# Compressed value products of two pairs in one group at the head of the sums, and the norms' epsilon on VectorE, in a two-layer hybrid decoder

## The chip, the cores and the metric

The kernel runs on one core of a Trainium2 chip. A core has a matrix engine (TensorE, PE in the rows), VectorE (DVE), ScalarE (ACT), GpSimd (POOL) and SyncE (SP), which here only issues transfers. Matrix products are written to PSUM, which has eight banks of 128 partitions by 512 float32; everything else works in SBUF. The metric is device time of one execution in microseconds; lower is better.

## The reference, cut to what matters

Two layers over 512 tokens of width 1024. In each, a projection feeds three mixers (a gated spatial MLP, a retention and a sparse attention), their outputs are joined and projected back, and a layer norm follows; then a gated feed-forward part with a short convolution, and a second layer norm. Two places bear on the change, the sum of three attention branches and the layer norm:

```python
o_cmp = jnp.einsum('bgrqk,bkgd->bqgrd', p_cmp.astype(dt), v_cmp)
...
o = gb[..., 0:1] * o_cmp + gb[..., 1:2] * o_sel + gb[..., 2:3] * o_win

def layer_norm(x, g, b):
    mu = jnp.mean(xf, axis=-1, keepdims=True)
    var = jnp.mean(jnp.square(xf - mu), axis=-1, keepdims=True)
    y = (xf - mu) * lax.rsqrt(var + LN_EPS)
    return (y * g.astype(jnp.float32) + b.astype(jnp.float32)).astype(x.dtype)
```

The compressed branch has 31 keys (padded to 32); the other two have up to 512. There are eight heads of width 64 in two groups of four.

## The kernel before, in words

Most products are made as three products of rounded halves (`mm3`, lines 449 to 453; `tm`, 538 to 546), which keeps float32 accuracy. TensorE's program runs through input projection, attention with retention between, output projection, the feed-forward part and the next layer. A scheduler of the framework orders each engine's instructions from the traced order, by readiness and free tiles; what is wrapped in `pin` keeps its traced place on its engine. All PSUM tiles come from one pool `ps` of eight banks.

**Attention** (`attention`, line 1045). The heads go in four pairs `hp` of two heads `e`; pairs 0 and 1 share key group `g` = 0, pairs 2 and 3 group 1. A pair has eight units (b, i): branch b (0 selected, 1 window) and token tile i of four. For a unit, `scores` makes the products with the keys, the mask, maximum, exp, sum and scale; it runs two units ahead (LOOK = 2) and takes two banks for tiles 2 and 3. `transposes` turns the probabilities and copies them to SBUF. After tile 3 of a branch, `pv_mm` (1027 to 1042) multiplies with the values into one bank `po` for the pair: head 0 on columns 0 to 63 of the array, head 1 on 64 to 127, all 128 rows (line 1032). After branch 1 it adds the compressed branch (line 1039): 64 rows of `PC[g]`, the transposed probabilities of the pair's two heads of four (rows 0 to 63 for the even pair, 64 to 127 for the odd one), with `vcs`, the compressed values with zero rows for the other head. That closes the sum, and ScalarE copies it out (`YC`, 1042). `po` is taken at unit 0 of each pair. Between the steps of attention a generator `filler` gives TensorE other work: the retention's projections and chunks, in layer 0 also the conditioning products (`ada_bank`, line 327), later the first output products.

**Norms.** `stats` (line 1179) combines the tile's statistics on VectorE (`bn_aggr`, 1181), adds EPS on GpSimd (1182) and raises to the power -1/2 on GpSimd (1183). It is called 16 times: four token tiles, two norms, two layers. After the output projection, `normalize` (1185) subtracts and scales in one VectorE instruction, and `to_h` (430) transposes the tile for the next products. In layer 0 GpSimd also issues the transfers of the next layer's conditioning weights (line 341) in that time.

**The end** (lines 1371 to 1386). In layer 1 the last six row blocks of the down projection run tile by tile: for each tile t, TensorE makes two halves of 512 columns (the last tile: 512, 256, 256), `piece` (1351) gates, adds and takes statistics on VectorE, then `stats` and `norm_out` (1361): one subtract with gain over all 1024 columns (1363), multiply and add in halves (1366), each followed by a transfer to the output (1367). All of VectorE's instructions there are pinned in traced order.

Of the kernel before, what the change touches and what calls it, by code (L numbers as in the profile page):

```python
# [14 lines left out]
OP = mybir.AluOpType  # L15
# [4 lines left out]
D = 1024  # L20
NT = S // P
# [127 lines left out]
def tile_trunk(ctx, tc, I, tab, out, layers=L):  # L149
# [368 lines left out]
    for l in range(layers):  # L518
# [501 lines left out]
        def transposes(i, pp, PT):  # L1020
            for e in range(2):
# [2 lines left out]
                    T.transpose(pb[:, j * P:(j + 1) * P], pp[e][:, j * P:(j + 1) * P], ident)  # L1024
                A.copy(PT[e][:, i:i + 3 * i + 1:3, :], pb[:, :(i + 1) * P].rearrange("p (j q) -> p j q", q=P))  # L1025

        def pv_mm(hp, b, PT, po):

            g = hp // 2
            for j in range(NT):  # L1030
                for e in range(2):
                    T.matmul(po[64 * e:64 * e + 64, j * P:], VS[:, b, j, 64 * g:64 * g + 64],  # L1032
                             PT[e][:, 4 * j:4 * j + NT - j, :].rearrange("p a q -> p (a q)"),
                             start=(b == 0 and j == 0), stop=False, tile_position=(0, 64 * e))
            if b == 0:
                return
            rs = slice(64 * (hp % 2), 64 * (hp % 2) + 64)
            for e in range(2):
                T.matmul(po[64 * e:64 * e + 64, :], vcs[rs, g, e, :], PC[g][rs], start=False, stop=True,  # L1039
                         tile_position=(64 * (hp % 2), 64 * e))  # L1040
            YC[hp] = pool.tile([P, 512], F32, tag="yc", name="yc", bufs=2)
            A.copy(YC[hp], po)

        def attention():
            units = [(hp, b, i) for hp in range(4) for b in range(2) for i in range(NT)]
            LOOK = 2
            pend = {}
            PT = po = None
            for u, (hp, b, i) in enumerate(units):
                for v in range(u, min(u + LOOK + 1, len(units))):  # L1050
                    if v not in pend:
                        h_, b_, i_ = units[v]
                        if i_ == 0 and not b_:
                            pend[v], pend[v + NT] = scores0(h_)
                        else:
                            pend[v] = scores(*units[v])
                if i == 0:
                    PT = [big("pT").rearrange("p (a q) -> p a q", q=P) for _ in range(2)]
                    if b == 0:
                        po = ps()  # L1060
                yield
                transposes(i, pend[u], PT)
                pend[u] = None
                yield
                if i == NT - 1:
                    pv_mm(hp, b, PT, po)
                    if b:
                        yield ("pair", hp)
# [110 lines left out]
        def stats(t, st, nst, dve=loose):  # L1179
            mv = pool.tile([P, 4], F32, tag="mv", name="mv", bufs=4)  # L1180
            dve(V.bn_aggr(mv[:, 0:2], st[:, :nst, :]))  # L1181
            G.tensor_scalar(mv[:, 2:3], mv[:, 1:2], EPS, None, op0=OP.add)  # L1182
            G.tensor_tensor(mv[:, 3:4], mv[:, 2:3], mhalf[:, 0:1], op=OP.pow)
            return mv

# [174 lines left out]

        def norm_out(t, mv):

            pin(V.scalar_tensor_tensor(X[t], X[t], mv[:, 0:1], lgr, op0=OP.subtract, op1=OP.mult))
            for c0, c1 in ((0, 512), (512, D)) if t < NT - 1 else ((0, 512), (512, 768), (768, D)):
                c = slice(c0, c1)
                pin(V.scalar_tensor_tensor(X[t][:, c], X[t][:, c], mv[:, 3:4], lbr[:, c], op0=OP.mult, op1=OP.add))
                nc.sync.dma_start(out[0, t * P:(t + 1) * P, c], X[t][:, c])
# [56 lines left out]
```

## Time and profile before

| what | value |
|---|---|
| median of 3 runs | 1386.84 us (1384.04 to 1389.21) |
| profiled execution, its own time | 1387.29 us |
| span from first to last instruction | 1385.5 us |
| TensorE busy | 1344.4 us, 97% |
| VectorE busy | 871.7 us, 63% |
| ScalarE busy | 545.0 us, 39% |
| GpSimd busy | 193.6 us, 14% |
| mean granted clock of TensorE | 0.994 |

All times of the trace count from the first instruction. A matrix product's record runs from issue to a modelled end and overlaps its followers, so spacing is read from starts. A float32 product is two instructions (two passes). GpSimd's spans are rough.

### The profile page before, as it was taken

How to read it: one execution, taken by the hardware profiler on the slowest of the kernel's cores; microseconds unless marked ns; L12 is line 12 of the kernel's file. 1: busy time of each engine (PE TensorE's matmuls, PEld its weight loads, DVE VectorE, ACT ScalarE, POOL GpSimd, SP SyncE). 2: the span in 40 equal slices, each digit the busy share in tenths (PEclk: the TensorE clock that was granted, in tenths of full speed). 3: DMA queues.
4: the chain of work that ended last, by engine and by line, in shares of the span. 5: the costliest groups of instructions: out<-in, count | busy, mean ns of one | idle time of the engine just before them, and what ended most of it. 6: DMA issues, size and time to landing. Idle time of an engine off the chain costs nothing.

```text
span 1385.5 us, 19644 instructions
## 1 busy us (share of the span) xinstructions
PE 1344.4 (97%) x7741; PEld 1107.8 (80%) x7741; DVE 871.7 (63%) x1436; ACT 545.0 (39%) x998; POOL 193.6 (14%) x196
## 2 busy tenths in 40 slices
PE   5999999999999999999999999999999999999996
PEld 4798665679987878778889988877998888888885
DVE  6668443756697776943567677475665555674347
ACT  3435333553433343332424354565343334343220
POOL 0311220334121120000000024112400000000002
PEclk9999999999999999999999999999999999999998
DMA  9822555512596674423525231111223333332221
GB/s 301 230 80 69 167 165 149 174 47 77 163 291 213 213 247 145 132 89 100 158 46 132 64 107 50 43 47 39 84 77 94 105 91 122 105 123 91 91 91 61
DMA packets 182328, 168.91 MB, mean 122 GB/s; under 512 B 23588, under 2 KB 161948, under 8 KB 182236
## 3 DMA queue, kind: packets, MB, share of 16 engines
q1 hardware_dynamic: 174684, 141.18, 34.8%
q0 software_dynamic: 7552, 26.48, 5.7%
q8 instruction: 61, 1.00, 0.3%
q14 instruction: 31, 0.25, 0.1%
HBM read 163.44 MB, written 2.10 MB: 119 GB/s over the span
## 4 chain that ended last, share of the span: by engine, by line
PE 85%; DVE 6%; DMA 3%; ACT 2%; POOL 1%; SPq 1%; issue 1%; POOLq 0%; DVEq 0%; ACTq 0%
PE ps L451 19%; PE ps L453 19%; PE ps L452 19%; PE ps L544 4%; PE ps L545 4%; PE ps L546 4%; PE ps L1032 3%; PE ps L327 2%; PE ps L1024 2%; DMA a<-in_w_ada_dram 1%; PE ps L973 1%; PE ps L974 1%; DMA wraw<-in_w_up_dram 1%; DMA wraw<-in_w_in_dram 1%; PE ps L1039 1%
## 5 line engine op out<-in xcount | busy, mean ns | idle before, releaser
L125 ACT CAST whi<-wraw 128x1024 fp32r<-128x1024 f32 (+4 forms) x183 | 181.5, 996 | 391.1 <-PE ps L452 235.5
L127 DVE TENSOR_TENSOR wlo<-wraw,whi 128x1024 fp32r<-128x1024 f32 (+3 forms) x157 | 181.6, 1162 | 160.9 <-ACT whi L125 157.6
L453 PE MATMUL ps<-h2h,wlo 128*128 128x512 f32 (+1 forms) x736 | 278.3, 378 | 0.0
L452 PE MATMUL ps<-h2l,whi 128*128 128x512 f32 (+1 forms) x736 | 277.2, 377 | 0.0
L451 PE MATMUL ps<-h2h,whi 128*128 128x512 f32 (+1 forms) x736 | 277.1, 377 | 0.0
L452 PEld LDWEIGHTS ps<-h2l,whi 128*128 128x128 f32 x736 | 138.2, 188 | 28.7 <-issue 1.7
L451 PEld LDWEIGHTS ps<-h2h,whi 128*128 128x128 f32 x736 | 138.2, 188 | 28.4 <-ACT whi L125 2.5
L453 PEld LDWEIGHTS ps<-h2h,wlo 128*128 128x128 f32 x736 | 138.3, 188 | 26.1 <-issue 0.8
L544 PE MATMUL ps<-whi,hh 128*128 128x256 f32 (+1 forms) x448 | 132.0, 295 | 0.0
L545 PE MATMUL ps<-wlo,hh 128*128 128x256 f32 (+1 forms) x448 | 129.1, 288 | 0.0
L546 PE MATMUL ps<-whi,hl 128*128 128x256 f32 (+1 forms) x448 | 127.2, 284 | 0.0
L452 PE MATMUL ps<-wlo,pt 128*128 128x512 f32 x256 | 101.4, 396 | 0.0
L451 PE MATMUL ps<-whi,pt 128*128 128x512 f32 x256 | 101.2, 396 | 0.0
L544 PEld LDWEIGHTS ps<-whi,hh 128*128 128x128 f32 x448 | 85.4, 191 | 13.9 <-issue 11.3
L453 PE MATMUL ps<-whi,pt 128*128 128x512 f32 x256 | 90.4, 396 | 0.0
L545 PEld LDWEIGHTS ps<-wlo,hh 128*128 128x128 f32 x448 | 85.4, 191 | 5.6 <-issue 5.3
L127 POOL TENSOR_TENSOR wlo<-wraw,whi 128x1024 fp32r<-128x1024 f32 x26 | 62.5, 2405 | 163.9 <-ACT whi L125 148.8
L546 PEld LDWEIGHTS ps<-whi,hl 128*128 128x128 f32 x448 | 85.3, 190 | 0.1
L1182 POOL TENSOR_SCALAR mv<-mv 128x1 f32<-128x1 f32 x16 | 9.0, 560 | 543.0 <-DVE mv L1181 543.0
L989 ACT ACTIVATE pt<-ps,sm 128x256 f32<-128x256 f32 (+2 forms) x96 | 55.8, 590 | 39.0 <-DVE sm L986 27.5
L1279 ACT ACTIVATE t<-ps,pcol 128x512 f32<-128x512 f32 x88 | 68.1, 774 | 0.9 <-PE ps L453 0.9
L1025 ACT COPY pT<-ps 128x128 f32<-128x128 f32 (+3 forms) x128 | 50.4, 437 | 44.1 <-PE ps L1024 43.6
(271 smaller groups left out, 2610.7 us busy)
## 6 DMA issues: line engine op xcount, KB each, us to landing
wraw<-in_w_up_dram SPq DMA_DIRECT2D x88, 512.0 KB, 3.8
araw<-in_w_ada_dram POOLq DMA_DIRECT2D x48, 512.0 KB, 5.2
wraw<-in_w_down_dram SPq DMA_DIRECT2D x44, 512.0 KB, 3.4
wraw<-in_w_ada_dram SPq DMA_DIRECT2D x32, 512.0 KB, 3.8
wraw<-in_w_in_dram SPq DMA_DIRECT2D x30, 512.0 KB, 3.9
wraw<-in_w_out_dram SPq DMA_DIRECT2D x16, 512.0 KB, 3.7
a<-in_w_ada_dram SPq DMA_DIRECT2D x14, 512.0 KB, 9.1
wraw<-in_w_in_dram SPq DMA_DIRECT2D x8, 384.0 KB
```

What stands on the lines that cost most here:

```text
L125: self.nc.scalar.copy(f(hi), src)
L127: eng.tensor_tensor(f(lo), src, f(hi).bitcast(F32), op=OP.subtract)
L451: at(T.matmul(o, lh, rh, start=first, stop=False))
L452: T.matmul(o, lh, rl, start=False, stop=False)
L453: T.matmul(o, ll, rh, start=False, stop=last)
L544: T.matmul(o, a, wh[:, k - k0, :], start=(first and k == 0), stop=False)
L545: T.matmul(o, a, wl[:, k - k0, :], start=False, stop=False)
L546: T.matmul(o, b, wh[:, k - k0, :], start=False, stop=(last and k == KD - 1))
L989: A.activation(pp[e][:, :n], o[e], AF.Exp, bias=sm[:, 0, e:e + 1], accum_out=sm[:, 1, e:e + 1])
L1025: A.copy(PT[e][:, i:i + 3 * i + 1:3, :], pb[:, :(i + 1) * P].rearrange("p (j q) -> p j q", q=P))
L1032: T.matmul(po[64 * e:64 * e + 64, j * P:], VS[:, b, j, 64 * g:64 * g + 64], PT[e][:, 4 * j:4 * j + NT - j, :].rearrange("p a q -> p (a q)" ...
L1279: A.activation(a, pa, AF.Identity, bias=cwc[:, 3, cx:cx + 1], scale=cwc[:, 2, cx:cx + 1])
```

## The change

It does three things.

A new function `pv_cmp` makes the compressed branch's products of both pairs of a key group: for each head e of a pair and each pair r, rows 64 r of the array and columns 64 e, into the two banks of the two pairs. It is called when the even pair begins, and its products open both sums; `pv_mm` then adds to them, and its last product closes the sum. The odd pair's bank is so taken a pair earlier.

In `stats`, VectorE adds EPS in place of GpSimd, pinned where `bn_aggr` is pinned. The power stays on GpSimd.

In `norm_out` the subtract is made in two halves of 512 columns.

```diff
+        def pv_cmp(hp):
+            g = hp // 2
+            po = [ps(), ps()]
+            for e in range(2):
+                for r in range(2):
+                    rs = slice(64 * r, 64 * r + 64)
+                    T.matmul(po[r][64 * e:64 * e + 64, :], vcs[rs, g, e, :], PC[g][rs], start=True, stop=False,
+                             tile_position=(64 * r, 64 * e))
+            return po
...
-                             start=(b == 0 and j == 0), stop=False, tile_position=(0, 64 * e))
+                             start=False, stop=(b == 1 and j == NT - 1), tile_position=(0, 64 * e))
             if b == 0:
                 return
-            rs = slice(64 * (hp % 2), 64 * (hp % 2) + 64)
-            for e in range(2):
-                T.matmul(po[64 * e:64 * e + 64, :], vcs[rs, g, e, :], PC[g][rs], start=False, stop=True,
-                         tile_position=(64 * (hp % 2), 64 * e))
...
                     if b == 0:
-                        po = ps()
+                        if hp % 2 == 0:
+                            pos = pv_cmp(hp)
+                        po = pos[hp % 2]
...
-            G.tensor_scalar(mv[:, 2:3], mv[:, 1:2], EPS, None, op0=OP.add)
+            dve(V.tensor_scalar(mv[:, 2:3], mv[:, 1:2], EPS, None, op0=OP.add))
...
-            pin(V.scalar_tensor_tensor(X[t], X[t], mv[:, 0:1], lgr, op0=OP.subtract, op1=OP.mult))
+            for c in (slice(0, 512), slice(512, D)):
+                pin(V.scalar_tensor_tensor(X[t][:, c], X[t][:, c], mv[:, 0:1], lgr[:, c], op0=OP.subtract, op1=OP.mult))
```

## Rows read from the trace of the kernel before

**Rows 1.** The page's first part: busy time, share and instructions of each engine.
```profile
PE 1344.4 (97%) x7741; PEld 1107.8 (80%) x7741; DVE 871.7 (63%) x1436; ACT 545.0 (39%) x998; POOL 193.6 (14%) x196
```

**Rows 2.** Stretches: length, busy time by engine, granted clock, DMA; three attention pairs.
```profile
124.00:180.00 56.00, 56.00 (x370) 39.66 (x370) 34.37 (x99) 24.04 (x73) 13.20 (x12) 1.00 0.44 129
...
238.00:278.00 40.00, 37.62 (x273) 25.81 (x269) 30.43 (x69) 21.65 (x60) 11.37 (x9) 0.96 0.52 163
...
907.00:937.00 30.00, 29.17 (x243) 22.92 (x241) 23.47 (x67) 19.04 (x57) 1.64 (x1) 1.00 0.13 35
```

**Rows 3.** Order of time (start, length): VectorE at the end's tile 0, TensorE's last product.
```profile
1351.49 0.21 DVE L1181 BATCH_NORM_AGGREGATE mv<-bst 128x2 f32<-128x12 f32 x1
1351.73 1.28 DVE L1363 SCALAR_TENSOR_TENSOR xa<-xa,mv,lg 128x1024 f32<-128x1024 f32 x1
1353.78 1.41 DVE L1366 SCALAR_TENSOR_TENSOR xa<-xa,mv,lb 128x512 f32<-128x512 f32 x2 [0.77 <-POOL mv L1183]
...
1374.22 0.28 PE L453 MATMUL ps<-wx,gt 128*128 128x256 f32 x1
```

**Rows 4.** GpSimd: its epsilon line's durations (ns, min/median/max), then order of time.
```profile
L1182 POOL TENSOR_SCALAR mv<-mv x16: 220/234/1313, 334.4 to 1377.1; 128x1 f32<-128x1 f32 x16
...
1351.79 1.31 POOL L1182 TENSOR_SCALAR mv<-mv 128x1 f32<-128x1 f32 x1 [339.59 <-DVE mv L1181]
...
1378.51 0.57 POOL L1183 TENSOR_TENSOR mv<-mv,mhalf 128x1 f32<-128x1 f32 x1
```

**Rows 5.** The launch line's queue instructions: durations in ns, first and last start.
```profile
L1420 POOLq DRAIN  x3: 46/98/6249, 1378.5 to 1385.2; - x3
L1420 SPq DRAIN  x3: 7/7/7, 1382.9 to 1385.0; - x3
```

**Rows 6.** Compressed products: all of the line (ns), then one group and its follower.
```profile
L1039 PE MATMUL ps<-pcT,vcs x32: 589/615/641, 179.6 to 968.7; 64*64 64x512 f32 x32
...
179.62 1.07 PE L1039 MATMUL ps<-pcT,vcs 64*64 64x512 f32 x4
180.63 0.39 PE L545 MATMUL ps<-wlo,hh 128*128 128x256 f32 x1
```

**Rows 7.** TensorE in order of time: retention's scores on two row halves, and the next line.
```profile
238.79 0.72 PE L921 MATMUL ps<-t 64*128 64x128 f32 x8
239.44 0.45 PE L930 MATMUL ps<-vb,rot 128*64 128x64 f32 x8
```

**Rows 8.** TensorE's wait in 262 to 266 (us, times, longest), and a stretch's clock.
```profile
PE ps L921 <- ACT pt L989: 1.0, 1, 1.0
...
265.43:268.84 3.41, 3.41 (x15) 2.69 (x15) 3.38 (x9) 0.90 (x3) 0.00 (x0) 0.50 0.44 149
```

**Rows 9.** A VectorE operation on eight columns (ns).
```profile
L476 DVE TENSOR_SCALAR nst<-nst x8: 158/168/171, 94.8 to 938.8; 128x8 f32<-128x8 f32 x8
```

**Rows 10.** GpSimd, VectorE, TensorE in order of time: norm of tile 2, layer 0.
```profile
345.75 1.20 POOL L341 DMA_DIRECT2D araw<-in_w_ada_dram  x2
346.97 0.66 POOL L1183 TENSOR_TENSOR mv<-mv,mhalf 128x1 f32<-128x1 f32 x1
...
345.98 1.20 DVE L127 TENSOR_TENSOR wlo<-wraw,whi 128x1024 fp32r<-128x1024 f32 x1
347.12 0.41 DVE L1175 TENSOR_TENSOR xa<-xa,t 128x256 f32<-128x256 f32 x1
...
349.09 0.33 PE L436 MATMUL ps<-tb,xa 128*128 128x128 f32 x1 [1.75 <-DVE xa L1187]
```

**Rows 11.** The end: TensorE leaves tile 2's second half, VectorE takes it.
```profile
1365.91 0.39 PE L451 MATMUL ps<-wx,pt 128*128 128x512 f32 x1
...
1366.34 0.67 DVE L1356 TENSOR_TENSOR t<-ps,grow 128x512 f32<-128x512 f32 x1
```

**Rows 12.** GpSimd's power on eight columns, and VectorE beside it, in layer 0.
```profile
102.00 1.65 POOL L477 TENSOR_TENSOR nst<-nst,mhalf 128x8 f32<-128x8 f32 x1 [4.51 <-DVE nst L476]
...
102.61 1.23 DVE L127 TENSOR_TENSOR wlo<-wraw,whi 128x1024 fp32r<-128x1024 f32 x1 [0.69 <-ACT whi L125]
```

## The prediction

> **What bounds the kernel now.** I read the page first: TensorE is busy for 97% of the span, every other engine for 63% or less [rows 1]. So an edit counts where it shortens TensorE's work, or where TensorE waits. Then the busy time by stretch: in the attention of layer 0 the first pair leaves TensorE no idle time at all, the third pair leaves 2.38 us of 40, and in layer 1 the third pair leaves 0.83 us of 30 [rows 2]. Last the end of the kernel, in order of time. There TensorE is done by 1374.5, and a chain on VectorE runs on: for each token tile bn_aggr (0.21), the subtract (1.28), an idle 0.77 until GpSimd's power has ended, and then the two final multiplies [rows 3]. GpSimd's queue also sets the very end: its drain starts at 1378.5 beside the last power and takes 6.25 us, to 1384.7, while SyncE's waits for the output are over at 1382.9 [rows 4, 5]. The last 0.8 us of the span is the closing handshake.
>
> **1. Value products of the compressed branch.** Before, each pair of heads (four in each of two layers: eight) closes its sum with a group of 64-row, 64-column products, 32 instructions in all, four a group [rows 6]. One group holds TensorE for 1.01 us, from 179.62 to the next instruction at 180.63 [rows 6]. Its two column halves already run together: four instructions of 0.59 us or more fit in 1.07, so their two passes start 0.48 apart. The change makes one group for two pairs, on both row halves, so four groups in place of eight. Changes of tile shape stay six for two pairs (before, three a pair; after, two a pair and two for the new group), so I take a group without its switch, 0.9 us, and not 1.01: 4 x 0.9 = 3.6 us off TensorE, between 3.6 and 4.0.
> This needs the two row halves to run at once. The trace has that in another place: retention's scores are eight instructions of 128 columns, four on each row half [rows 7]. By the spacing above, 128 columns take 0.48 / 4 = 0.12 us, so eight in line would need 0.96; the next line starts after 0.65, switch included. They overlap. The two halves write different banks there, as they will here. What no row shows is four 64 x 64 tiles at once; bounds 0 and 4.0, value 3.6, since row halves and column halves each overlap alone.
>
> **2. A PSUM bank more, held for a pair.** The sum of the second pair of a group is opened with the first's, so in the first and third pair of each layer two of the eight banks are held by sums where one was. Look-ahead scores (two banks a unit), transposes and the filler share them. If a bank isn't free, the next scores wait, and TensorE idles only when the filler can't go either. Nearest rows: the idle time of the two third pairs, 2.38 and 0.83 us, and the clock, which was granted at half (1.2 GHz) for 3.41 us after waits such as the 1.0 us of retention's scores for an exp, which cost 1.7 us of work [rows 2, 8]. Ends: nothing (the first pair of layer 0 has none to lose) and the same again, 3.2 + 1.7 = 4.9. Below nothing is possible too: another order may miss the clock's fall (a gain of 1.7). In these pairs ACT and VectorE, not TensorE, also hold some of the gain of point 1. I take +1.2 us for both.
>
> **3. Epsilon on VectorE, and the subtract in halves, at the end.** Why is the idle 0.77? GpSimd's epsilon on one column takes 0.22 us alone, but 1.31 here [rows 4]: it starts at 1351.79, inside VectorE's subtract (two operands in SBUF, 1351.73 to 1353.01), and ends 0.09 after that. Only then comes the power, 0.57. After the change, counted from bn_aggr's start: epsilon at 0.24 for 0.17 (a column operation of its kind [rows 9]), done at 0.41; first half of the subtract at 0.33, since an instruction that needs nothing of its forerunner starts 0.08 before that ends (two multiplies of 0.75 in 1.41 [rows 3]), to 1.08; second half 1.00 to 1.75; the multiply could start at 1.67. The power is released at 0.41 + 0.09 = 0.50, inside the first half. Row for what follows: at 346.97 a power started under a VectorE instruction with two SBUF operands (345.98 to 347.18), another such followed from 347.12 to 347.53, and the power ended at 347.63 [rows 10]: 0.45 after the first one's end. A power alone takes 0.57 and the blocked epsilon needed 0.09 after its release, so a power let in only at 347.53 would hardly be done 0.10 later. I read it as let in between the two, and the second one (0.41) was not drawn out. Here then: 1.08 + 0.45 = 1.53, ahead of 1.67. The multiply comes 1.67 after bn_aggr instead of 2.29: 0.62 us for each of four tiles. The second instruction's own cost, 0.13 (1.41 against 1.28), is in that.
> What is late next: after two tiles VectorE would be 1.24 ahead and want the second half of tile 2 at 1365.10, but TensorE leaves that bank at 1365.91, and VectorE could start some 0.2 later; before, it started at 1366.34 [rows 11]. So 0.24 of 1.24 is left; tile 2's own norm adds 0.62, making 0.86. In tile 3 only the power matters, because GpSimd's drain follows it: its end moves from just ahead of 2.29 to 1.53 after bn_aggr, some 0.73. SyncE's path moves by 0.86 + 0.62 and keeps over 1.5 us of slack. Sum 0.86 + 0.73 = 1.6 us; ends 0.3 (first rival) and 2.1 (with TensorE no bound).
> One row speaks on the other order, too: in layer 0 a power ran from 102.00 to 103.65, and a VectorE subtract with both operands in SBUF started inside it, at 102.61, and took 1.23, where another took 1.20 [rows 10, 12]. A running power did not hold VectorE up to its end. The Trainium skill, "SBUF — State Buffer", section "SBUF: two separate sides", calls the port pair that GpSimd and VectorE share an exclusive lock: whichever starts first keeps it for its whole instruction, and the other blocks fully. The epsilon that waited out the subtract agrees with it; the subtract inside the power does not. By that rule the second half would wait for the power's end.
>
> **4. Epsilon elsewhere.** Twelve other norms swap GpSimd's 0.22 and two hand-overs (about 0.09 each) for 0.17 on VectorE, ahead of whatever is queued there; TensorE waits for a norm in one place only, 1.75 us before 349.09 [rows 10]. There GpSimd's queue holds two DMA issues (345.75, 1.20 us) between epsilon and power. Once epsilon is gone from that queue, the power may go ahead of them (a gain up to 1.7, all of the wait) or stay behind (nothing; 0.2 lost if epsilon queues behind VectorE's next subtract). Value 0.5. The 16 x 0.17 = 2.7 us on VectorE are covered by its idle time; at the end they are in point 3.
>
> **Sum.** -3.6 + 1.2 - 1.6 - 0.5 = -4.5 us. The profiled execution took 1387.29 (span 1385.5), 0.45 above the median 1386.84; on the median: 1382.3.
>
> **Rivals.**
> First, the halves don't help: the power is let in after the first but keeps the second out until it ends (1.53; second half to 2.28, multiply at 2.20), or it is let in only after both (1.75 + 0.45 = 2.20, multiply 2.23). Either way 0.06 to 0.09 a tile is gained, and the last power ends 0.06 to 0.73 earlier: the end gives 0.3 to 1.0 instead of 1.6. Time 1382.9 to 1383.6. For it: the 1.31 of [rows 4]; against it: [rows 10, 12]. The Trainium skill's section named in point 3 would give the first form. Chance 0.10.
> Second, the row halves of the new group run in line. Point 1 then gives 0: 1385.9. For it: no row with four tiles; against: [rows 7]. Chance 0.05.
> Third, slower: the missing bank. Place: the first and third pairs of both layers, 32 units; price: an idle of the kind in layer 0's third pair, 2.4 us a pair beyond today's (point 2 with the half clock: up to 4.1). It decides once it passes the 3.6 + 1.6 + 0.5 = 5.7 gained elsewhere, that is 1.4 us a pair. With 2.4 in each of four pairs: 9.6 - 5.7 = +3.9, 1390.7; with 4.1: 1397.5. For it: retention's chunks take up to five banks there and TensorE already idles; against it: filler covers both first pairs. Chance 0.18, of which half lies beyond 1393.8.
> Fourth, better: banks cost nothing, and the power passes the DMA issues: -3.8 - 1.6 - 1.7 = -7.1, 1379.7; 1378.0 if the clock's fall goes too. Chance 0.12.
> The forecast has the remaining 0.55.
>
> **Range and chances.** 1379 to 1389 leaves out the far half of the third rival and the clock's part of the fourth. 0.5% is 6.9 us, about what a measurement of this kernel can tell from no change: faster means below 1379.9 (most of the fourth rival and an edge of the forecast, 0.15), slower above 1393.8 (0.09), same 0.76.
>
> **What would show it.** In the changed profile: the new line with 32 instructions in four groups of eight, each about 1.0 us from first start to the next line (in line: 1.9); the pairs' stretches each shorter by a part of 0.9 us, or idle time and half clock in first and third pairs (third rival); bn_aggr to multiply 1.67 us, the power's span about 1.0 and VectorE's idle there near nothing (2.2: first rival); VectorE waiting for TensorE once, before tile 2's second half; GpSimd's drain ending as far after the power as before; and TensorE's 1.75 before 349. A sum of attention's gain below 2 us with no idle time there would make point 1 wrong; an end that doesn't move with the last power makes point 3's drain wrong.

## The result and the profile after

The changed kernel is slower: 1398.72 us median of six runs (1397.99 to 1401.54) against 1387.24 for the kernel before beside it, a ratio of 1.009 with a 95% interval of 1.0074 to 1.0105. That is over the 0.5% of the forecast's bounds and 9.7 us above the top of its range (1389). The profiled execution took 1398.53 (span 1396.8, mean granted clock 0.994), 11.3 us of span more than before at the same mean clock.

The table gives the length of each stage and what each kernel adds to it, by the profiled executions; the pairs are cut at the starts of ScalarE's copies that end them (line 1042 before, 1049 after). The last four columns are kernels of the section on the experiments. The profiled execution of before (1387.29) is longer than the medians of before beside the experiments (1383.5 to 1385.9), so the columns of the experiments come out some 2 to 3 us lower than their medians do: e17 has +2.9 us of span here and +5.6 by the medians.

| stage, us | before | after | e1 | e14 | e16 | e17 |
|---|---|---|---|---|---|---|
| start, to the compressed branch | 116.3 | -0.3 | -0.8 | -2.6 | -1.1 | +0.4 |
| layer 0, first pair | 64.4 | +0.9 | 0 | +0.7 | 0 | 0 |
| second pair | 58.2 | +1.3 | 0 | -1.5 | +1.5 | 0 |
| third pair | 39.5 | +5.2 | -0.4 | +2.3 | +5.4 | -3.3 |
| fourth pair | 31.2 | +2.3 | 0 | 0 | +2.0 | +1.9 |
| to the first norm's start | 23.8 | +0.6 | -0.4 | -0.1 | -0.8 | +0.6 |
| first norm | 16.9 | +1.1 | +0.8 | +0.7 | +0.3 | +0.4 |
| feed-forward, to layer 1's attention | 463.1 | -0.8 | -1.0 | -1.0 | -0.1 | -0.2 |
| layer 1, first pair | 53.5 | -0.6 | 0 | -0.5 | 0 | 0 |
| second pair | 40.7 | -0.7 | 0 | -0.9 | 0 | 0 |
| third pair | 30.4 | +0.5 | 0 | 0 | +1.4 | -0.1 |
| fourth pair | 31.3 | +2.0 | 0 | 0 | +1.9 | +2.1 |
| output projection, norm, feed-forward | 382.1 | +1.5 | +0.4 | +0.6 | +0.1 | +1.1 |
| the last tiles | 25.3 | -0.9 | -0.9 | -0.9 | 0 | 0 |
| from the last norm to the end | 8.7 | -0.8 | -0.8 | -0.8 | 0 | 0 |

The end gained what was forecast. The loss lies in attention, 7.5 of the 11.3 us in layer 0's third and fourth pairs, 2.2 in its first two and 2.0 in layer 1's fourth.

The page's first line for the engines, which answers to [rows 1]: TensorE is busy 3.3 us longer, though the same number of instructions runs on it; the other 8 us are idle time. Read from the spacing of starts, the compressed products hold TensorE 2.1 us less than before, but the conditioning products (line 327) 2.8 us more (33.3 against 30.5), all of it in layer 0's third and fourth pairs, and the transposes of the probabilities 1.2 us more.

```profile
PE 1347.7 (96%) x7741; PEld 1107.2 (79%) x7741; DVE 878.6 (63%) x1456; ACT 545.9 (39%) x998; POOL 185.8 (13%) x180
```

The busy time by stretches of attention (length, busy time of TensorE, its weight loads, VectorE, ScalarE, GpSimd, TensorE's granted clock, DMA share, GB/s); of before, for layer 0's last two pairs and layer 1's last two:

```profile
239.00:310.00 71.00, 67.12 (x475) 48.68 (x474) 46.43 (x104) 40.58 (x105) 20.52 (x14) 0.98 0.34 105
907.60:969.30 61.70, 59.02 (x446) 45.66 (x445) 39.93 (x103) 37.50 (x101) 10.41 (x6) 1.00 0.12 34
```

The same of after, and the first two pairs of each layer:

```profile
240.80:319.00 78.20, 70.40 (x475) 48.99 (x476) 46.96 (x104) 40.55 (x104) 19.67 (x13) 0.98 0.33 100
916.60:980.80 64.20, 58.66 (x445) 46.09 (x444) 40.24 (x104) 37.73 (x102) 10.40 (x5) 1.00 0.13 35
116.00:240.80 124.80, 124.80 (x785) 84.89 (x784) 58.53 (x148) 48.89 (x139) 24.04 (x19) 1.00 0.45 134
823.70:916.60 92.90, 92.90 (x686) 79.35 (x684) 57.94 (x142) 51.21 (x141) 29.39 (x18) 1.00 0.18 53
```

In the first two pairs TensorE has no idle time (124.80 of 124.80, 92.90 of 92.90): the filler covers everything there. (Layer 0's are 2.2 us longer all the same; 1.5 of it is compressed products, of which more lie in them.) In the last two it idles 7.80 us in layer 0 where it idled 3.88, and 5.54 in layer 1 where it idled 2.68. The mean clock of these stretches is what it was.

TensorE's waits from 110 to 1030 (what waited and for what; us in all, times, longest). Before, then after:

```profile
PE ps L1024 <- DVE pt L993: 2.9, 3, 1.4
PE ps L1032 <- ACT pT L1025: 2.3, 4, 0.8
PE ps L436 <- DVE xa L1187: 1.9, 2, 1.7
...
PE ps L452 <- POOL wlo L127: 1.1, 2, 0.5
PE ps L921 <- ACT pt L989: 1.0, 1, 1.0
PE ps L1082 <- DVE gb L955: 0.4, 1, 0.4
```

```profile
PE ps L436 <- DVE xa L1196: 3.6, 2, 2.2
PE ps L1024 <- ACT pt L989: 3.5, 3, 1.6
PE ps L452 <- POOL wlo L127: 3.2, 2, 1.6
PE ps L1091 <- DVE gb L955: 3.1, 2, 1.6
PE ps L921 <- ACT t L913: 2.4, 3, 1.7
PE ps L1043 <- ACT pT L1025: 2.3, 2, 1.1
```

Two kinds are new. Inside the pairs, the transposes of the probabilities (L1024) now wait 3.5 us for the exp itself, where they waited 2.9 for the scaling behind it, and retention's scores (L921) wait 2.4 for the copy of their turned queries and keys, where they waited 1.0 for an exp. Behind the pairs, the output product's wait for GpSimd's split of the weights (L452) and that of the transposes of the joined outputs (1082 before, 1091 after) for VectorE grew by 2.1 and 2.7 us: that is where products of the compressed branch stood before. The norm's transposes (L436) wait 1.7 us more.

### The profile page after: what moved, and what is told of

It is laid out like the page before. It is cut to its first block, busy times and chain, and to the rows that moved or that the text cites. A ratio compares the mean times of both kernels' runs of the same rounds, so it can differ in the third digit from the quotient of the medians.

```text
span 1396.8 us, 19640 instructions
## 1 busy us (share of the span) xinstructions
PE 1347.7 (96%) x7741; PEld 1107.2 (79%) x7741; DVE 878.6 (63%) x1456; ACT 545.9 (39%) x998; POOL 185.8 (13%) x180
## 4 chain that ended last, share of the span: by engine, by line
PE 87%; DVE 6%; DMA 3%; issue 2%; POOL 1%; SPq 1%; ACT 1%; DVEq 0%; POOLq 0%; ACTq 0%
PE ps L451 20%; PE ps L452 20%; PE ps L453 20%; PE ps L544 4%; PE ps L545 4%; PE ps L546 4%; PE ps L1043 3%; PE ps L327 2%; PE ps L1024 2%; DMA a<-in_w_ada_dram 1%; PE ps L973 1%; PE ps L974 1%; PE ps L436 1%; DMA wraw<-in_w_in_dram 1%; PE ps L514 1%
## 5 line engine op out<-in xcount | busy, mean ns | idle before, releaser
L125 ACT CAST whi<-wraw 128x1024 fp32r<-128x1024 f32 (+4 forms) x183 | 181.4, 995 | 391.4 <-PE ps L452 233.8
L452 PE MATMUL ps<-h2l,whi 128*128 128x512 f32 (+1 forms) x736 | 277.2, 377 | 0.0
L452 PEld LDWEIGHTS ps<-h2l,whi 128*128 128x128 f32 x736 | 138.2, 188 | 28.7 <-issue 1.7
L452 PE MATMUL ps<-wlo,pt 128*128 128x512 f32 x256 | 101.5, 397 | 0.0
L1192 POOL TENSOR_TENSOR mv<-mv,mhalf 128x1 f32<-128x1 f32 x16 | 11.3, 705 | 551.9 <-DVE mv L1191 551.9
L989 ACT ACTIVATE pt<-ps,sm 128x256 f32<-128x256 f32 (+2 forms) x96 | 55.7, 588 | 63.0 <-DVE sm L986 49.6
L1290 DVE SCALAR_TENSOR_TENSOR t<-ps,pcol,t 128x510 f32<-128x510 f32 x88 | 65.5, 746 | 2.1
```

The source lines that it names most:

```text
L125: self.nc.scalar.copy(f(hi), src)
L452: T.matmul(o, lh, rl, start=False, stop=False)
L989: A.activation(pp[e][:, :n], o[e], AF.Exp, bias=sm[:, 0, e:e + 1], accum_out=sm[:, 1, e:e + 1])
L1290: V.scalar_tensor_tensor(a[:, 2:], pa[:, :-2], cwc[:, 0, cx:cx + 1], a[:, 2:], op0=OP.mult, op1=OP.add)
```

## The experiments

**Which part.** e1 makes only the norms' part of the change, e2 only the joint group.

```diff
# e1
-            G.tensor_scalar(mv[:, 2:3], mv[:, 1:2], EPS, None, op0=OP.add)
+            dve(V.tensor_scalar(mv[:, 2:3], mv[:, 1:2], EPS, None, op0=OP.add))
...
+            for c in (slice(0, 512), slice(512, D)):
...
# e2
...
+                        if hp % 2 == 0:
+                            pos = pv_cmp(hp)
+                        po = pos[hp % 2]
```

> The kernel before, with VectorE adding epsilon and the last norms' subtract in halves; the attention is untouched. If the bank held a pair early is what costs (bank theory), this one is faster than before by the end's part alone: 1.0 to 2.5 us, ratio 0.998 to 0.9995, bn_aggr to multiply 1.67 us instead of 2.29, and the attention's stretch as before within 1 us. If epsilon on VectorE is what costs (norm theory), it is slower by several us, with TensorE waiting for norms after the output projections.

Measured: 1384.8 against 1385.94, 0.999 (0.998 to 1.0).

> The kernel before, with the compressed group of two pairs opening both sums; epsilon and subtract as before. Bank theory: the whole loss and the end's gain missing, so 12 to 14 us slower than before, ratio 1.009 to 1.010, with the idle time before the transposes of layer 0's third pair as in the changed kernel. Norm theory: 1 to 4 us faster than before, since only TensorE's 3.6 us are left.

Measured: 1399.48 against 1385.94, 1.0098 (1.0082 to 1.0114). The whole loss comes with the joint group; the norms' part gains 1.1 us by the medians, at the edge of its interval.

**Which pairs.** e12 has the norms' part and joins only the first two pairs of layer 1; e14 the norms' part and the first two pairs of both layers. The others close their sums as before.

```diff
+        def joint(hp):
+            return l == 1 and hp < 2        # e12
+            return hp < 2                   # e14
...
+                        if joint(hp) and hp % 2 == 0:
+                            pos = pv_cmp(hp)
+                        po = pos[hp % 2] if joint(hp) else ps()
```

> The norms' part of the change everywhere, and the joint group only for pairs 0 and 1 of layer 1, where the filler covers a missing bank; everywhere else the groups close their sums as before. Bank and cover theories: 1.3 us gained in layer 1's first two pairs, 1.2 to 2.9 by the norms, so 2.5 to 4 us faster than before and 1 us faster than e1. Order theory: slower than e1 by several us.

Measured: 1383.32 against 1383.9, 0.999 (0.9977 to 1.0002). No loss, but not the 2.5 to 4 us either.

> The whole change for the norms, and the joint group for pairs 0 and 1 of both layers; the groups of pairs 2 and 3 close their sums as before. Bank and cover theories: layer 1 gains 1.4 us as with the joint group there alone; layer 0 loses the 2.2 us of its first two pairs (conditioning products no longer four at a time) and nothing in the third and fourth, so 0 to 3 us slower than the kernel with the group in layer 1 alone, and 8 us or more faster than the changed kernel. If a new order costs wherever it is, the third and fourth pair of layer 0 lose 3 us or more too.

Measured: 1382.56 against 1384.18, 0.9987 (0.9974 to 1.0). So the loss sits wholly in the group for pairs 2 and 3. Where both pairs are filled, the joint group does no harm, and with the norms' part it is as fast as any version here, though its gain of 1.6 us is at the edge of what these runs tell from none. (Of its +2.3 in layer 0's third pair at most 1.7 goes with a clock at half for some 7 us there, from 254 to 261, against 3.4 before.)

**What the products are worth.** e9 leaves the compressed branch's products out altogether, e10 those of pairs 2 and 3.

```diff
-            for e in range(2):
+            for e in range(2 if hp < 2 else 0):   # e10; e9: no products at all
                 T.matmul(po[64 * e:64 * e + 64, :], vcs[rs, g, e, :], PC[g][rs], ...
```

> The kernel before without any compressed value products (that branch is left out of the sum), so 8 x 1.0 us less on TensorE and nothing moved. If TensorE bounds the whole attention: 7 to 9 us faster. Cover theory (the groups that close pairs 2 and 3 stand in waits that other engines end, so taking them away only lengthens the waits): 3 to 5 us faster, and the waits for the retention's norm and for GpSimd's weight split are 1.0 us longer in each layer. Order theory (any new order of TensorE's instructions costs): slower than before.

Measured: 1386.93 against 1383.9, 1.0023 (1.0011 to 1.0035).

> The kernel before without the compressed products of pairs 2 and 3 alone (left out of the sum), 4 us less on TensorE. TensorE-bound: 3.5 to 4.5 us faster. Cover theory: within 1.5 us of before, with the waits ahead of the output transposes and the output projection 1.0 us longer. Order theory: 3 us or more slower.

Measured: 1387.66 against 1383.9, 1.0028 (1.0013 to 1.0043). Both missed the times of the cover theory, though the waits that it named did grow, and came out as the order theory had it. Eight microseconds of TensorE's work are gone in e9, and the kernel is 3 us slower by the medians (its profiled execution is 1.1 us shorter than that of before). Some 2 of the 3 us go with the clock, by an estimate from the mean granted clock of the runs, 0.9932 against 0.9947; so the least that is shown is that the 8 us gained nothing. In the first and second pairs of both layers each group gave back about what it took (-1.0, -1.1, -1.0, -1.0), but not later: the third and fourth pairs together are 0.7 longer in layer 0 and 0.1 in layer 1. TensorE's waits of e9, same stretch and columns:

```profile
PE ps L436 <- DVE xa L1183: 3.6, 3, 2.3
...
PE ps L452 <- POOL wlo L127: 3.2, 2, 1.6
PE ps L1078 <- DVE gb L955: 2.3, 2, 1.4
```

The output product after the last pair waits 1.6 for GpSimd in each layer, as in after, and 0.5 before: the 1.0 us of products that closed the fourth pair stood inside a wait that GpSimd ended anyway. L1078 (the 1082 of before) and the norm's transposes (L436) lengthened in the same way.

**The bank alone.** e5 takes one more bank at unit 0 of every pair and frees it after the first branch's last tile. e16 does so in pairs 2 and 3 only, with the bank time that the change has there: two banks from the start of pair 2, one freed in the first half of each pair. Both keep all of the kernel's products where they were and add some that nobody uses (estimated at 0.6 us of work in e16 and 1.5 in e5; by the spacing of starts e16's hold TensorE for 1.1).

```diff
# e5, at unit 0 of each pair
+                        idle = ps()
+                        T.matmul(idle[:, :16], ident, ident[:, :16], start=True, stop=True)
...
# e16
+                        if hp == 2:
+                            idle = [ps(), ps()]
...
+                    if b == 0 and hp > 1:
+                        V.tensor_tensor(seen, idle[hp - 2][:, 0:1], PT[1][:, 3, 0:1], op=OP.add)
```

> The kernel before, products as they were; beside them each pair takes one more bank at its first unit (16 columns of a product that nobody uses) and lets it go when the first branch's probabilities of tile 3 have been copied, which is the time by which the opened sums of e3 hold theirs earlier. It adds about 1.5 us of small work. Bank theory: slower than before by 6 to 11 us, as e3 (8.5), with the same traces: conditioning products less often four at a time, longer waits ahead of the output projection. Place theory (the products' own place in TensorE's order costs): within 3 us of before.

Measured: 1392.82 against 1383.51, 1.0058 (1.0036 to 1.008): 9.3 us, as the bank theory had it.

> The kernel before, its products as they were, with the change's bank time in pairs 2 and 3 alone: two idle banks are taken at the third pair's first unit (16 columns each, unused), one let go when the third pair's own sum opens, one when the fourth's does. 0.6 us of added work. If the bank carries the loss of pairs 2 and 3: 8 to 13 us slower, with the waits of retention's scores and chunk products in layer 0's third pair. If the lost cover carries it: within 2 us of before.

Measured: 1397.75 against 1384.75, 1.0094 (1.0074 to 1.0113). Holding the banks is enough for the whole loss, 13.0 us, without any product moved. The added instructions held no engine up: TensorE was not idle before them, and VectorE for at most 0.03 us before each of the four that let the banks go. A run that adds them and lets the banks go at once was not made. The stages agree: +5.4 and +2.0 in layer 0's last pairs (after: +5.2 and +2.3), +1.9 in layer 1's fourth (after: +2.0). Its stretches, columns as above:

```profile
239.30:317.50 78.20, 70.89 (x473) 49.71 (x474) 47.70 (x106) 40.54 (x105) 20.35 (x14) 0.96 0.31 98
914.90:979.90 65.00, 60.22 (x445) 45.76 (x446) 41.35 (x105) 37.67 (x102) 10.46 (x6) 1.00 0.13 37
```

The idle time is 7.31 and 4.78 us, near that of after. The clock, 0.96 against 0.98, was granted at half for some 7 us here against 3.4 in after; at most 1.7 of the third pair's 5.4 us is the clock's. Its waits, from 238 to 325:

```profile
PE ps L921 <- ACT t L913: 1.9, 1, 1.9
PE ps L1032 <- ACT pT L1025: 1.9, 2, 1.1
PE ps L1024 <- DVE state L949: 0.9, 1, 0.9
PE ps L1024 <- ACT pt L989: 0.9, 1, 0.9
```

These include the kinds of after inside the pairs (L921, L1024). The waits behind the pairs have hardly grown: the wait for GpSimd's split stays at 0.5 a layer, and that of the transposes of the joined outputs is 0.6, since e16 keeps the closing products.

**The opening alone.** In e3 each pair's own group opens its sum at the pair's start. In e4 both pairs' own groups stand at the even pair's start. In e6 each pair's own group opens the sum just ahead of its first value products, so its bank is taken at most 2 us earlier. e17 does that in pairs 2 and 3 only.

```diff
# e3
-                        po = ps()
+                        po = pv_own(hp)
# e4
+                        if hp % 2 == 0:
+                            pos = [pv_own(hp), pv_own(hp + 1)]
# e6 (e17: if b == 0 and hp > 1), in pv_mm ahead of the value products
+            if b == 0:
+                pv_own(hp, po)
```

> The kernel before, but each pair's own compressed products open the pair's sum, where before they closed it: eight groups as before, no bank taken earlier. Bank theory: the time of before within 3 us. If the place at the head of the sum is what costs (place theory: products early in TensorE's order, ahead of scores that are due), 5 to 12 us slower.

Measured: 1394.43 against 1385.94, 1.0073 (1.0051 to 1.0096): 8.5 us, which the place theory had and the bank theory, in this form, did not.

> As the run before it, but the odd pair's sum is opened already at the start of the even pair, by its own products, so a second bank is held for a pair and nothing is packed on row halves. Bank theory: slower than the run before it by 8 to 15 us. Place theory: within 3 us of the run before it. If two row halves packed together are what costs (packing theory), also within 3 us of it, and only the run with the joint group is slow.

Measured: 1399.55 against 1385.94, 1.0096 (1.0076 to 1.0116), 5.1 above the run before it where the bank theory had 8 to 15. Its four tiles ran together too, since the two groups came to stand side by side; so it can't tell banks from packing.

> Each pair's own products open the sum, but just ahead of the pair's first value products, so the bank is taken when it was before. Bank theory: the time of before within 3 us. Place theory (opening itself costs): 5 to 12 us slower. If any new order of TensorE's instructions costs (order theory: the order of before is a lucky one), slower by several us too, with no bank taken earlier.

Measured: 1389.91 against 1383.51, 1.0047 (1.0031 to 1.0063): 6.4 us, which the place and order theories had and the bank theory did not.

> The kernel before, where pairs 2 and 3 alone open their sums with their own products just ahead of their first value products (the bank taken at most 2 us earlier), so the groups leave the ends of these pairs and nothing is held. If the lost cover carries the loss: 4 to 8 us slower, with the waits for the retention's norm and for GpSimd's weight split 1.0 us longer in each layer. If the bank does: within 2 us of before.

Measured: 1390.38 against 1384.75, 1.0041 (1.0024 to 1.0058): 5.6 us, as the lost cover had it. Two things follow. The cost rises with the time that banks are held: 6.4 us by the medians in e6, where hardly any is, 8.5 in e3, 13.6 and 13.5 in e4 and e2 (the intervals of neighbours overlap, those of e6 and of e4 and e2 do not). And taking the products away from the pairs' ends costs something with no bank held. In e17's trace the clock did not fall in attention, and still its span is 2.9 longer; its stretches:

```profile
239.30:308.70 69.40, 66.21 (x480) 47.49 (x481) 43.22 (x104) 40.12 (x105) 20.42 (x13) 1.00 0.33 106
907.50:971.20 63.70, 58.91 (x452) 45.94 (x452) 39.87 (x103) 37.51 (x102) 10.78 (x5) 1.00 0.11 32
```

The fourth pair is 1.9 and 2.1 longer in the two layers, as in after. So each of the two causes lengthens the fourth pair by about 2 us, and the change, which has both, shows 2.3 and 2.0: they do not add up. In layer 0's third pair only the bank costs (e16 +5.4, e17 -3.3).

**The order of the products.** e13 is the change with the group's products kept in their traced order. e7 puts the joint group behind the even pair's last value products, e8 is e7 with the norms' part.

```diff
# e13
+                    (pin if e or r else loose)(
+                        T.matmul(po[r][64 * e:64 * e + 64, :], vcs[rs, g, e, :], PC[g][rs], start=True, stop=False,
# e7, e8, at the end of the even pair's pv_mm
+                for e in range(2):
+                    for r, (o, first) in enumerate(((po, False), (odd, True))):
```

> The changed kernel with the joint group's products kept in their traced order behind each other, so that in layer 0 the second group (issued in three pieces, 3.0 us) may stand together (1.0 us). If the split carries the loss: 2 us or more faster than the changed kernel. Bank theory: the pieces stood apart because the second bank was not free, so together they start later, and the time stays within 2 us of the changed kernel (11 to 13 us above before).

Measured: 1397.8 against 1384.18, 1.01 (1.0078 to 1.0122). Other lines' products still came between those of layer 0's second group (starts at 234.97, 237.96 and 241.25), so it decides nothing on the split.

> The joint group of two pairs stands behind the even pair's last value products: it closes the even pair's sum and opens the odd one's, whose bank is then taken half a pair earlier than before, in odd pairs only. Epsilon and subtract as before. Bank theory: a quarter of the bank time of the changed kernel, so about 3.5 us lost and 3 to 5 gained by packing (1.0 to 1.25 a group): -3 to +2 us against before. Order theory: 5 to 12 us slower like the others.

Measured: 1395.49 against 1383.51, 1.0075 (1.0049 to 1.0101): 12.0 us. The bank theory's -3 to +2 missed this run by the most; the order theory had 5 to 12.

> The run before it with epsilon on VectorE and the subtract in halves. The norms' part gave 1.2 us in e1 (2.9 in its profiled execution), so 1 to 3 us below the run before it by every theory, if the attention keeps its order; bank theory: -6 to 0 us against before.

Measured: 1393.51 against 1383.51, 1.0074 (1.0051 to 1.0097): 2.0 below e7, as forecast, and 10.0 above before, where the bank theory had at most 0. The scheduler issued the two halves of each group apart (in e7's first group at 174.8 and 181.4), so the four tiles never ran together and nothing was packed; the odd pair's bank was again held ahead of time.

e11 and e15 move no compressed product; they only take the two heads in the other order, in the transposes (e11) and in the value products (e15).

```diff
# e11 line 1021, e15 line 1031
-            for e in range(2):
+            for e in (1, 0):
```

> The kernel before with the two heads of a unit transposed in the other order: no bank taken earlier, no product moved to another place, the same work. Bank and cover theories: within 2 us of before. Order theory (the order of before is a lucky one and any other costs): 4 us or more slower.

Measured: 1389.84 against 1383.9, 1.0039 (1.0022 to 1.0056): 5.9 us, as the order theory had it.

> The kernel before with the two heads' value products in the other order (second head first), otherwise nothing changed: no bank, no moved product. Bank and cover theories: within 2 us of before. Order theory: 4 us or more slower, as with the heads' transposes in the other order (5.4).

Measured: 1381.58 against 1384.18, 0.999 (0.9969 to 1.0012): not the order theory's 4 us or more. But neither run is the equal work that it was meant to be. In before the value products of a pair's two heads mostly start apart; in e11 and e15 each second head's product starts 7 ns behind the first's, on the other column half. The value products of before, then of e11 (count, then busy us and mean ns, then idle time before them):

```profile
L1032 PE MATMUL ps<-pT,vs 128*64 128x128 f32 (+3 forms) x256 | 52.2, 441 | 2.4 <-ACT pT L1025 2.3
L1032 PE MATMUL ps<-pT,vs 128*64 128x512 f32 (+3 forms) x256 | 39.7, 453 | 6.8 <-ACT pT L1025 6.8
```

They take 12 us less of TensorE (39.9 in e15), and in e11 TensorE's waits from 110 to 1030 grow from 11 to 25 us. e11 also has a lower mean granted clock over its runs, 0.9894 against 0.9947, which is 7.3 us of 1385 by an estimate from these two, more than its loss; e17 has none of this (0.9949 against 0.9943), e16 some 1 us (0.9935 against 0.9943). In e11's trace the first two pairs are shorter and both fourth pairs over 3 us longer (+3.1 and +3.3, at most 1.7 of it the clock's in each), with no bank held and no product moved; so some of the 2 us in the fourth pairs of e16 and e17 may be what any new order costs there.

**Banks or order.** The runs that hold no bank early and yet change something in the third and fourth pairs cost 3.0 to 6.4 us (e6, e9, e10, e11, e17), all but e15; that is the order theory's rival, and no run prices it by itself. The traces tell the two apart all the same. The wait of the transposes for the exp, L1024 for L989 in after, comes to 1.7 to 3.5 us in all nine traces where a bank is held early in those pairs (after, e2, e3, e4, e5, e7, e8, e13, e16) and to at most 0.2 in the ten others. The nine are 8.5 to 13.6 us slower than before, the others at most 6.4. The scores' wait for the copy (L921) doesn't tell them apart: e6 has 2.8 us of it.

## Why the prediction was wrong, and where it was right

**Point 1: the packing was right, its worth was not.** Four 64 x 64 tiles do run at once. TensorE of after, in order of time (start, length), first group of layer 0; layer 0's second group:

```profile
126.46 1.09 PE L1034 MATMUL ps<-pcT,vcs 64*64 64x512 f32 x8
127.48 0.39 PE L544 MATMUL ps<-whi,hh 128*128 128x256 f32 x1
...
234.40 1.08 PE L1034 MATMUL ps<-pcT,vcs 64*64 64x512 f32 x4
235.40 1.04 PE L327 MATMUL ps<-wraw,ce 128*32 128x512 f32 x2
236.38 1.07 PE L1043 MATMUL ps<-pT,vs 128*64 128x512 f32 x2
237.38 1.07 PE L1034 MATMUL ps<-pcT,vcs 64*64 64x512 f32 x2
238.38 2.37 PE L1043 MATMUL ps<-pT,vs 128*64 128x512 f32 x14
240.68 1.07 PE L1034 MATMUL ps<-pcT,vcs 64*64 64x512 f32 x2
```

Eight instructions take 1.02 us (126.46 to 127.48), as four did before [rows 6]; that is "about 1.0 us from first start to the next line", and the second rival falls. Two things of the step failed. First, one group of the four was not issued as a group. The scheduler let other products in between, and the three pieces hold TensorE for 1.00, 1.00 and 0.99 us. So layer 0's groups take 4.02 us where they took 4.02, and only layer 1's fell, from 4.10 to 2.04. The prediction took four whole groups for granted. Second, it priced every microsecond off TensorE at a microsecond, "3.6 us off TensorE". The 97% of [rows 1] is an average. In layer 1's first two pairs, which are full, the change gained 1.3 (forecast for two pairs: 0.9), 0.5 of it idle time of before. At the end of the third and fourth pairs TensorE was waiting for others, and the removed group came back as a wait: 0.54 to 1.58 before the output product in layer 1. By e9 and e10 the products there were worth nothing to begin with; by e17, moving them costs about 5.6, part of which may be the price of any other order.

**Point 2 is the term that was mis-sized**: +1.2 of 0 to 4.9, where e16 measures 13.0 for the bank time of pairs 2 and 3 alone. It went wrong in two places. The count of held banks was wrong: "in the first and third pair of each layer two of the eight banks are held by sums where one was". The source takes the tile at a pair's first unit, but nothing is written to it until its first product. In before the third pair's bank of layer 0 begins with the first value product at 256.29, 17 us after the pair's start at 238.9; in after it begins at 234.40. If a bank counts from its first product on, the change lengthens every pair's own hold by about half a pair and adds the odd pair's on top. e3, which adds no second bank, would have cost nothing by the prediction's count, and it cost 8.5; but e6, with hardly any bank time, already cost 6.4, so the cleaner number is e5's, 9.3 for one more bank in half of each pair with no product moved. No run shows by itself when the scheduler counts a bank as taken. And the price was taken from idle time that was already there ("the same again"), though that shows how long TensorE waits with eight banks and not how much worse it gets with fewer. By this reading, where the filler is thin, a bank less means that less work stands between a unit's exp and its transposes, and TensorE waits in several places at once; the wait of the transposes for the exp, which only the runs with a bank held early have, fits that, and no run shows a bank's wait itself, since it is settled in the order of the instructions. What the clock's 1.7, the other half of the upper end, was worth stays open. e1's trace has no fall of the clock in attention, and its third pair in layer 0, with the same products, is only 0.4 shorter; but of the 33 runs of before beside e9 the 13 with a mean clock of 0.994 took 1386.6 us on average, the 16 with 0.995 1383.4 and the 4 with 0.996 1381.2.

**The third rival** named the mechanism, gave it 1390.7 to 1397.5 and a chance of 0.18; the result, 1398.72, lies just beyond. Its reason against itself held (the filler covers both first pairs), as e14 shows; its place was half right: the third and the fourth pairs, not the first and third.

**Point 3 was right.** VectorE at tile 0 of the end, in order of time, answering to [rows 3]; then GpSimd's power, of after:

```profile
1364.42 0.21 DVE L1190 BATCH_NORM_AGGREGATE mv<-bst 128x2 f32<-128x12 f32 x1
1364.66 0.15 DVE L1191 TENSOR_SCALAR mv<-mv 128x1 f32<-128x1 f32 x1
1364.74 1.41 DVE L1373 SCALAR_TENSOR_TENSOR xa<-xa,mv,lg 128x512 f32<-128x512 f32 x2
1366.06 1.41 DVE L1376 SCALAR_TENSOR_TENSOR xa<-xa,mv,lb 128x512 f32<-128x512 f32 x2
...
1379.04 0.69 DVE L1365 TENSOR_TENSOR t<-ps,grow 128x512 f32<-128x512 f32 x1 [1.01 <-PE ps L453]
```

```profile
1364.96 0.93 POOL L1192 TENSOR_TENSOR mv<-mv,mhalf 128x1 f32<-128x1 f32 x1 [340.34 <-DVE mv L1191]
...
1389.41 0.93 POOL L1192 TENSOR_TENSOR mv<-mv,mhalf 128x1 f32<-128x1 f32 x1 [6.73 <-DVE mv L1191]
```

The multiply comes 1.64 after bn_aggr (forecast 1.67, before 2.29) with no idle time between. The power takes 0.93 (forecast "about 1.0"), and VectorE then waits for TensorE once, 1.01 before tile 2's second half. The last tiles gained 0.9 (0.86) and the end 0.8 (0.73), 1.7 in all against 1.6; e1, e12 and e14 show the same two numbers. GpSimd's drain still sets the end, and it ends as far after the last power as before, 5.64 us, as the prediction asked. Its rows, as in [rows 5]:

```profile
L1430 POOLq DRAIN  x3: 46/93/6591, 1389.4 to 1396.5; - x3
```

The first rival falls: the power started at 1364.96 inside the first half and was done at 1365.89, while the second half ran to 1366.15 without a pause. The Trainium skill, "SBUF — State Buffer", section "SBUF: two separate sides", has whichever engine of the shared pair starts first keep the other out for its whole instruction. That the power took 0.93, where the shortest power of this line took 0.55, agrees with a hold by the first half; that the second half then ran beside it does not.

**Point 4 was right at its one place, and not in sum**: in e1 the wait ahead of tile 2's transposes [rows 10] went from 1.75 to 1.15, a gain of 0.6 against the 0.5 taken; GpSimd's two DMA issues stayed ahead of the power there, and only the epsilon left the queue.

```profile
347.33 1.09 PE L436 MATMUL ps<-tb,xa 128*128 128x128 f32 x8 [1.15 <-DVE xa L1187]
```

But the same wait in layer 1, which the prediction left out, went from 0.17 (at 1007.19) to 0.60 (at 1005.90), so 0.2 of the gain is left in e1. In after the two waits are 2.20 and 1.38; in e17, with epsilon on GpSimd and the late products moved, they are 2.26 and 0.99.

**What stays open.** How much of the loss in layer 0 is due to the split of its second group (2.0 us of TensorE's time, at the seam of two pairs) was not isolated, nor how much is the price of any new order in the third and fourth pairs. Nor is it settled wait by wait why the two causes, 13.0 and 5.6 alone, give 11.5 together with gains of some 1.6 from e14's part. That they lengthen the same fourth pairs by the same 2 us says that they overlap there, and no more.

## What to carry to other kernels

Before moving a product to the head of a sum, count from when its PSUM tile is first written: opening a sum early holds a bank for the whole time until the old first product, and where a pool of eight is shared by look-ahead work this can cost several times what it saves (here 13.0 us in e16, against 3.6 hoped for). Price a microsecond of the busiest engine by what ends the wait next to it: in a full stretch it was worth a microsecond (e9's first two pairs), ahead of a wait on another engine nothing. When a gain is local, make the change only in the stretches that are full (here the first two pairs of each layer), and see that what is meant to run together is issued together.

## What the runs showed of the hardware

Four float32 products on 64 x 64 tiles of the array, two of them to each of two banks, start 6 to 7 ns apart and take 1.02 us for all eight passes, as long as two tiles did. Value products of two heads on the two column halves start 7 ns apart when they stand next to each other, and all 256 then take 39.7 us where they took 52.2 (e11); the time came back as waits. Taking 8 us of work off an engine that is 97% busy gained nothing (e9). The clock's fall to half at 265 before [rows 8] is no fixed feature: it is absent from the traces of e1 and e17, and e11 and e15, which only swap two heads, show falls at 298 and 943, or at 299, 930 and 957 besides. The runs of e15 differ with the clock: the four at 0.987 or 0.988 took 1387.3 us on average, the five at 0.992 or 0.993 1379.9. GpSimd's closing drain began beside its last power and ended 5.64 us after that power's end, in before and in after; it took 6.59 us against 6.25 because the power inside it took 0.93 against 0.57.
